# Hybrid decoder layer on one core: a two-tile first weight block on its own queue, and the third out chunk's h transposed on TensorE

## The chip, the cores and the metric

One core of one Trainium2 chip runs the kernel. The metric is the device time in microseconds (us) of one execution; the time given for a kernel is the median of several runs. Five engines work side by side: TensorE (PE in the profile; PEld is its weight load), VectorE (DVE), ScalarE (ACT), GpSimd (POOL) and SyncE (SP), which here only issues DMAs. All transfers run on the 16 DMA engines of the core.

## The reference

One decoder layer on x of 256 tokens by 2048 channels, float32: forgetting attention (16 heads of 128) behind an RMS norm, then a gated MLP with a causal convolution of width 3 behind another.

```python
h = x
a = rms_norm(h, mix_norm)                      # h * rsqrt(mean(h*h) + eps) * gain
q, k, v, f_logit = split(a @ fox_w_in)         # 2048 -> 3 * 2048 + 16
...
h = h + attention(q, k, v, f_logit) @ fox_w_out
up = rms_norm(h, ffn_norm) @ ffn_w_up          # 2048 -> 2 * 5632
y = causal_conv3(up)
gate, val = split(y)
h = h + (silu(gate) * val) @ ffn_w_down        # 5632 -> 2048
```

## The kernel before

Every matmul runs on split operands: a float32 number is taken as hi + lo, both of a type that TensorE multiplies at full rate, and three products hi\*hi, hi\*lo and lo\*hi are added up in PSUM. `split_load` (L157) makes this of a weight block: one DMA on SP's queue into `raw` (4 buffers), a cast on ScalarE to `hi` (L167), a subtraction on VectorE to `lo` (L168; 5 buffers each of hi and lo, 1024 columns wide, so two k tiles of 512 columns). `halves` (L214) does the same for activations, with the norm's gain of the channel as a factor: ScalarE (L215), then VectorE (L216). The factor of the RMS norm for each token is applied to the results.

The input side. x stands transposed in memory (`xT`), 16 k tiles of 128 channels by 256 tokens. The first chunk of products, `q0` (heads 12 to 15 of q, 512 columns), walks over the 16 k tiles; its weights come in blocks of 1, 1, 2, 2, ... k tiles (L40). `q_first` runs ahead of each block: it issues the load of the block's x (`x_load`, L193, SP's queue) and makes `xs[k]` from it (`x_make`, L220). The gains of both norms, as 32 columns, come first of all by a DMA on ScalarE's queue (L140). Each k tile has 6 products: for each of two token tiles, hi\*hi (L353), hi\*lo (L354) and lo\*hi (L355). The `k0` chunk follows on the same xs.

The middle. The output projection has four chunks of 512 columns (`out_part`, `out_evac`). Chunk c is added to the residual `res` (L306), and its 512 channels, 4 k tiles of the next norm's input `hs`, must be transposed. For chunks 0 to 2 VectorE transposes blocks of 32 by 32 (L315), 16 DMAs on GpSimd's queue move the blocks (`spread`, L258; 48 in all) into `hT`, and `scale` makes the halves of hs (L324, L325). For chunk 3 `h_turn` (L223) transposes on TensorE (8 transposes of 128 by 128 for the four k tiles, L228, into PSUM), and `halves` reads PSUM. `bg` is a list of such jobs that `tick` takes one from, every second k tile in the out chunks and twice in each quarter of an up half.

The up projection (`up_half`) then has 11 blocks of a gate half (`pug`) and a value half (`puv`), each in four quarters of 4 k tiles: 16 products of 512 columns (L278), then 16 of 256 (L280). Quarter i needs hs[4i] to hs[4i+3]. In the first block the job `spread_rstd` adds a few small products (tile `prb`, L643).

What sets the order: the program gives priorities, and a planner with its own model of durations puts the instructions of each engine into a fixed order (`schedule_with_timeline_sim`). Each engine then runs its list in order, and waits where an input or a buffer isn't ready.

Of the kernel before, what the change touches and what calls it, by code (L numbers as in the profile page):

```python
# [9 lines left out]
F32 = mybir.dt.float32  # L10
F32R = mybir.dt.float32r
AF = mybir.ActivationFunctionType
ALU = mybir.AluOpType
AX = mybir.AxisListType

P = 128
S = 256
SQ = 32
NT = S // P
D = 2048  # L20
KT = D // P
# [7 lines left out]
HEL = 1024  # L29
# [6 lines left out]
def plan_in():  # L36
    r = {}
    for g, (h0, nh) in enumerate(GROUPS):
        q, k, v = (list(range(m * D + h0 * HD, m * D + (h0 + nh) * HD)) for m in range(3))
        r[f"q{g}"] = (q, [1, 1] + [2] * 7 if g == 0 else [4] * 4)  # L40
        r[f"k{g}"] = (k, [4] * 4)
        if g == 0:

            r["v0a"] = (v[0 : 2 * HD] + list(range(3 * D, 3 * D + NH)), [6, 6, 4])
            r["v0b"] = (v[2 * HD :], [8, 8])
        else:
            r[f"v{g}"] = (v, [4] * 4)
    return r
# [46 lines left out]
def trunk_kernel(  # L95
# [1 line left out]
    tc: tile.TileContext,  # L97
    x: bass.AP,
    xT: bass.AP,
    cols: bass.AP,  # L100
    g_qk: bass.AP,
    w_in: bass.AP,
    b_f: bass.AP,
# [6 lines left out]
    nc = tc.nc  # L110
# [13 lines left out]
    bg = deque()  # L124
# [12 lines left out]
    make_identity(nc, ident)  # L137

    gains = const.tile([P, 2 * KT], F32, name="gains")
    nc.scalar.dma_start(gains, cols)  # L140
    gmix, gffn = gains[:, 0:KT], gains[:, KT : 2 * KT]
    gqk = const.tile([P, 2 * HD], F32, name="gqk")
    neghalf = const.tile([P, 16], F32, name="neghalf")
# [12 lines left out]

    def split_load(src, kk, n, name):  # L157
        raw = wraw.tile([P, WEL], F32, tag="raw", name=f"raw_{name}")
        nc.sync.dma_start(raw[:, 0 : kk * n], src)
        hv, lv = [], []  # L160
        step = max(1, HEL // n)
        for j in range(0, kk, step):
            w = min(step, kk - j)
            hi = whi.tile([P, HEL], F32R, tag="hi", name=f"hi_{name}_{j}")
            lo = wlo.tile([P, HEL], F32R, tag="lo", name=f"lo_{name}_{j}")
            src = raw[:, j * n : (j + w) * n]
            nc.scalar.copy(hi[:, 0 : w * n], src)  # L167
            nc.vector.tensor_tensor(  # L168
                lo[:, 0 : w * n], src, hi[:, 0 : w * n].bitcast(F32), op=ALU.subtract
            )  # L170
            hv += [hi[:, i * n : (i + 1) * n] for i in range(w)]
            lv += [lo[:, i * n : (i + 1) * n] for i in range(w)]
        return hv, lv
# [5 lines left out]
    xs = [acts.tile([P, 2, S], F32R, tag=f"as{k}", name=f"xs{k}") for k in range(KT)]  # L179
# [6 lines left out]
        nc.gpsimd.tensor_tensor(dst, dst, neghalf[:, 0:cols], op=ALU.pow)  # L186

    xv = x.rearrange("o (t p) d -> p (o t) d", p=P)
    xTv = xT.rearrange("p (k s) -> p k s", s=S)
    xq = [acts.tile([P, 2, S], F32, tag=f"os{i}", name=f"xq{i}") for i in range(KT // 2)]  # L190

    def x_load(k, w):
        nc.sync.dma_start(xq[k // 2][:, k % 2 : k % 2 + w, :], xTv[:, k : k + w, :])  # L193


    def res_load(c, late):
# [17 lines left out]
    def halves(dst, src, g):  # L214
        nc.scalar.activation(dst[:, 0, :], src, AF.Copy, scale=g)  # L215
        nc.vector.scalar_tensor_tensor(  # L216
            dst[:, 1, :], src, g, dst[:, 0, :].bitcast(F32), op0=ALU.mult, op1=ALU.subtract,
        )

    def x_make(k):  # L220
        halves(xs[k], xq[k // 2][:, k % 2, :], gmix[:, k : k + 1])

    def h_turn(kp):  # L223
        pt = bank(f"ht{kp}")
        for j in range(2):
            for t in range(NT):
                k = 2 * kp + j
                nc.tensor.transpose(  # L228
                    pt[:, j * S + t * P : j * S + (t + 1) * P], res[:, t, k * P : (k + 1) * P], ident,
                )  # L230
        for j in range(2):
            k = 2 * kp + j
            halves(hs[k], pt[:, j * S : (j + 1) * S], gffn[:, k : k + 1])
# [69 lines left out]
    def out_evac(pts, c):  # L303
        for t in range(NT):
            hc = res[:, t, c * 512 : (c + 1) * 512]
            nc.vector.tensor_tensor(hc, hc, pts[t], op=ALU.add)  # L306
            sq = hp_.tile([P, 512], F32, tag="hsq", name=f"hsq{c}_{t}")
            square(sq, t, c)
        if c == 3:
            bg.extend([nop, lambda: [h_turn(kp) for kp in (6, 7)]])  # L310
            return
        hq = tp.tile([P, 4 * NT, P], F32, tag="hq", name=f"hq{c}")
        hT = tp.tile([P, NT, 4, P], F32, tag="hT", name=f"hT{c}")
        for t in range(NT):
            nc.vector.transpose(  # L315
                hq[:, 4 * t : 4 * t + 4, :].rearrange("p k s -> p (k s)"), res[:, t, c * 512 : (c + 1) * 512]
            )
        spread(hT.rearrange("p t k s -> p (t k) s"), hq, nc.gpsimd)

        def scale():  # L320
            for j in range(4):
                k = 4 * c + j
                g, d = gffn[:, k : k + 1], hs[k].rearrange("p a (t s) -> p a t s", t=NT)
                nc.scalar.activation(d[:, 0], hT[:, :, j, :], AF.Copy, scale=g)  # L324
                nc.vector.scalar_tensor_tensor(  # L325
                    d[:, 1], hT[:, :, j, :], g, d[:, 0].bitcast(F32), op0=ALU.mult, op1=ALU.subtract,
                )

        bg.extend([nop] * (4, 3, 6)[c] + [scale])

    with tc.tile_pool(name="att", bufs=2) as att, tc.tile_pool(name="ckp", bufs=1) as ckp:
        scr = dram.tile([NH, S], F32, name="scr")
# [4 lines left out]
        def chunk(name, pre=None):  # L337
            cols, kbs = plan[name]
            n = len(cols)
            pts = [bank(f"p{name}_{t}", "mm") for t in range(NT)]  # L340
            k0 = 0
            lv = None
            for bi, kk in enumerate(kbs):
                if pre:
                    pre(bi, lv)
                hv, lv = split_load(wi[name, k0], kk, n, f"{name}_{bi}")
                for j in range(kk):
                    k = k0 + j
                    for t in range(NT):
                        o = pts[t][:, 0:n]  # L350
                        ah = xs[k][:, 0, t * P : (t + 1) * P]
                        al = xs[k][:, 1, t * P : (t + 1) * P]
                        nc.tensor.matmul(o, lhsT=ah, rhs=hv[j], start=(k == 0), stop=False)  # L353
                        nc.tensor.matmul(o, lhsT=ah, rhs=lv[j], start=False, stop=False)  # L354
                        nc.tensor.matmul(o, lhsT=al, rhs=hv[j], start=False, stop=(k == KT - 1))  # L355
                    if (k + 1) % (2 if n > 256 else 4) == 0:
                        tick()
                k0 += kk
            last[0] = lv[-1]
            return pts  # L360
# [198 lines left out]
        for g, (h0, nh) in enumerate(GROUPS):  # L559
            qd = {}  # L560
# [6 lines left out]


            def q_first(bi, lv):
                if bi < 2:  # L570
                    x_load(bi, 1)
                    x_make(bi)
                else:
                    k = 2 * (bi - 1)
                    x_load(k, 2)
                    x_make(k)
                    x_make(k + 1)
# [49 lines left out]
    for c in range(2, 4):  # L627
        pts = [bank(f"po_{c}_{t}", "mm") for t in range(NT)]
# [163 lines left out]
```

## Time and profile before

| | us |
|---|---|
| median of 3 runs | 1122.23 (1120.85 to 1123.55) |
| the profiled execution's own time | 1121.05 |
| its span, first to last instruction | 1119.3 |
| TensorE busy in it | 1110.5 (99%) |
| VectorE, ScalarE, GpSimd busy | 753.2, 570.5, 87.6 |

The chain of work that ended last is 96% TensorE. How to read the rows: a timeline row has start, duration, engine, line, operation, output<-inputs, shapes and how many instructions were merged; in brackets the idle time of that engine before it, and what ended it. SPq and ACTq are the queues on which SP and ScalarE issue DMAs. A matmul's duration reaches past the start of the next, since they are pipelined: the price of one in a dense row is the distance of the starts.

### The profile page before, as it was taken

Reading aid. Unit: us, or ns where it says so; the run is one execution under the profiler, and the core shown is the slowest. Engines: PE = TensorE matmul, PEld = TensorE weight load, DVE = VectorE, ACT = ScalarE, POOL = GpSimd, SP = SyncE. Lnnn points to the kernel's source line nnn. Section 1 sums busy time; section 2 is a strip of 40 time slices with the busy share of each in tenths; the row PEclk is TensorE's granted clock in tenths of the full one; section 3 lists DMA queues with packets and bytes.
Section 4 is the critical chain, followed back from the end, with each engine's and each line's share of the span. In section 5 each row is a group of like instructions: output and inputs, shape, how many; then the busy total and the mean of one; then the engine's idle time right before and its main releaser. Section 6 shows DMA issues by size and latency. Waiting matters only on the chain.

```text
span 1119.3 us, 15032 instructions
## 1 busy us (share of the span) xinstructions
PE 1110.5 (99%) x5672; PEld 950.0 (85%) x5672; DVE 753.2 (67%) x1210; ACT 570.5 (51%) x837; POOL 87.6 (8%) x152
## 2 busy tenths in 40 slices
PE   8999999999999999999999999999999999999998
PEld 6898888888888888888888888888888888888886
DVE  6666948677647658687655767765577777557864
ACT  7644545454535656565444555543455554346542
POOL 1102403030106400000000000000000000000000
PEclk9999999999999999999999999999999999999999
DMA  9839577677648645555555555555555555555542
GB/s 336 312 76 357 140 264 224 176 266 209 217 157 239 215 168 188 189 188 190 197 200 171 196 192 192 193 201 188 188 188 188 189 188 193 197 183 183 198 176 75
DMA packets 89145, 223.51 MB, mean 200 GB/s; under 512 B 58624, under 2 KB 58912, under 8 KB 64752
## 3 DMA queue, kind: packets, MB, share of 16 engines
q1 hardware_dynamic: 86640, 218.52, 57.8%
q0 software_dynamic: 2288, 4.01, 1.5%
q8 instruction: 44, 0.72, 0.2%
q14 instruction: 29, 0.24, 0.1%
q10 hardware_dynamic: 144, 0.02, 0.0%
HBM read 212.28 MB, written 2.11 MB: 192 GB/s over the span
## 4 chain that ended last, share of the span: by engine, by line
PE 96%; SPq 1%; DMA 1%; DVE 1%; ACT 0%; issue 0%; DVEq 0%
PE pug L278 14%; PE puv L278 14%; PE puv L280 8%; PE pug L280 7%; PE pd L290 7%; PE pd L289 7%; PE pd L291 7%; PE po L291 3%; PE pk L355 3%; PE pk L354 3%; PE po L290 3%; PE po L289 3%; PE pk L353 3%; PE pq L354 2%; PE pq L355 2%; PE pq L353 2%
## 5 line engine op out<-in xcount | busy, mean ns | idle before, releaser
L278 PE MATMUL puv<-hs,hi_uv 128*128 128x512 f32 x704 | 168.8, 391 | 1.2 <-ACT hi_uv L167 1.1
L278 PE MATMUL pug<-hs,hi_ug 128*128 128x512 f32 x704 | 167.9, 391 | 0.0
L168 DVE TENSOR_TENSOR lo_ug<-raw_ug,hi_ug 128x1024 fp32r<-128x1024 f32 x88 | 106.1, 1221 | 81.1 <-PE puv L280 36.8
L168 DVE TENSOR_TENSOR lo_d<-raw_d,hi_d 128x1024 fp32r<-128x1024 f32 x88 | 106.6, 1223 | 78.6 <-ACT hi_d L167 56.1
L278 PEld LDWEIGHTS puv<-hs,hi_uv 128*128 128x128 f32 x704 | 129.2, 188 | 26.9 <-ACT hi_uv L167 1.6
L278 PEld LDWEIGHTS pug<-hs,hi_ug 128*128 128x128 f32 x704 | 129.6, 188 | 25.2
L167 ACT CAST hi_d<-raw_d 128x1024 fp32r<-128x1024 f32 x88 | 92.2, 1052 | 114.8 <-PE pd L291 83.0
L167 ACT CAST hi_uv<-raw_uv 128x1024 fp32r<-128x1024 f32 x88 | 92.4, 1051 | 106.7 <-PE pug L278 63.2
L167 ACT CAST hi_ug<-raw_ug 128x1024 fp32r<-128x1024 f32 x88 | 92.6, 1052 | 105.9 <-PE puv L278 34.4
L168 DVE TENSOR_TENSOR lo_uv<-raw_uv,hi_uv 128x1024 fp32r<-128x1024 f32 x88 | 106.2, 1221 | 58.5 <-PE pug L280 47.2
L290 PE MATMUL pd<-lo_d,gt 128*128 128x512 f32 x352 | 136.2, 389 | 0.0
L289 PE MATMUL pd<-hi_d,gt 128*128 128x512 f32 x352 | 134.5, 389 | 0.0
L291 PE MATMUL pd<-hi_d,gt 128*128 128x512 f32 x352 | 134.2, 389 | 0.0
L280 PEld LDWEIGHTS puv<-hs,lo_uv 128*128 128x128 f32 x704 | 90.3, 191 | 3.4
L280 PEld LDWEIGHTS pug<-hs,lo_ug 128*128 128x128 f32 x704 | 90.3, 191 | 3.4
L280 PE MATMUL puv<-hs,lo_uv 128*128 128x256 f32 x704 | 91.5, 283 | 0.0
L280 PE MATMUL pug<-hs,lo_ug 128*128 128x256 f32 x704 | 91.3, 283 | 0.0
L291 PEld LDWEIGHTS pd<-hi_d,gt 128*128 128x128 f32 x352 | 66.1, 188 | 13.7
L289 PEld LDWEIGHTS pd<-hi_d,gt 128*128 128x128 f32 x352 | 66.1, 188 | 13.6
L290 PEld LDWEIGHTS pd<-lo_d,gt 128*128 128x128 f32 x352 | 66.1, 188 | 13.6
L168 DVE TENSOR_TENSOR lo_o<-raw_o,hi_o 128x1024 fp32r<-128x1024 f32 x32 | 39.1, 1222 | 34.2 <-ACT hi_o L167 33.8
L168 DVE TENSOR_TENSOR lo_q<-raw_q,hi_q 128x1024 fp32r<-128x1024 f32 (+1 forms) x33 | 38.8, 1187 | 27.0 <-ACT hi_q L167 27.0
(171 smaller groups left out, 1816.7 us busy)
## 6 DMA issues: line engine op xcount, KB each, us to landing
raw_ug<-in_w_up SPq DMA_DIRECT2D x44, 1024.0 KB, 4.9
raw_uv<-in_w_up SPq DMA_DIRECT2D x44, 1024.0 KB, 4.9
raw_d<-in_w_down SPq DMA_DIRECT2D x44, 1024.0 KB, 4.8
raw_k<-in_w_in SPq DMA_DIRECT2D x16, 1024.0 KB, 8.8
raw_o<-in_w_out SPq DMA_DIRECT2D x16, 1024.0 KB, 5.6
raw_q<-in_w_in SPq DMA_DIRECT2D x12, 1024.0 KB, 6.0
raw_v<-in_w_in SPq DMA_DIRECT2D x12, 1024.0 KB, 5.7
raw_q<-in_w_in SPq DMA_DIRECT2D x7, 512.0 KB, 6.8
```

Of the source, the lines that this page charges most:

```text
L167: nc.scalar.copy(hi[:, 0 : w * n], src)
L168: nc.vector.tensor_tensor(lo[:, 0 : w * n], src, hi[:, 0 : w * n].bitcast(F32), op=ALU.subtract)
L278: nc.tensor.matmul(o[:, 0:512], lhsT=hv, rhs=a.rearrange("p a s -> p (a s)"), start=first, stop=False)
L280: nc.tensor.matmul(o[:, 0:S], lhsT=lv, rhs=a[:, 0, :], start=False, stop=last)
L289: nc.tensor.matmul(pts[t], lhsT=ah, rhs=hv, start=first, stop=False)
L290: nc.tensor.matmul(pts[t], lhsT=ah, rhs=lv, start=False, stop=False)
L291: nc.tensor.matmul(pts[t], lhsT=al, rhs=hv, start=False, stop=last)
L353: nc.tensor.matmul(o, lhsT=ah, rhs=hv[j], start=(k == 0), stop=False)
L354: nc.tensor.matmul(o, lhsT=ah, rhs=lv[j], start=False, stop=False)
L355: nc.tensor.matmul(o, lhsT=al, rhs=hv[j], start=False, stop=(k == KT - 1))
```

## The change

The first weight block of `q0` holds two k tiles and comes by ScalarE's queue; it is split one k tile at a time. `xT` now begins with one block of 32 columns of gains and x of k tiles 0 and 1, loaded by one DMA on SP's queue into `xg`; the DMA of the columns is gone, and GpSimd copies them out of `xg`. The halves of `xs[0]` are both made on VectorE. In k tile 0 the products are in the order hi\*hi, lo\*hi, hi\*lo, each for both token tiles. Chunk 2 of the output projection goes the way of chunk 3: no block transposes and no DMAs, but `h_turn(4)` and `h_turn(5)` as a job behind one empty job.

```diff
--- before.py
+++ after.py
@@ -37,7 +37,7 @@
     r = {}
     for g, (h0, nh) in enumerate(GROUPS):
         q, k, v = (list(range(m * D + h0 * HD, m * D + (h0 + nh) * HD)) for m in range(3))
-        r[f"q{g}"] = (q, [1, 1] + [2] * 7 if g == 0 else [4] * 4)
+        r[f"q{g}"] = (q, [2] * 8 if g == 0 else [4] * 4)
         r[f"k{g}"] = (k, [4] * 4)
         if g == 0:
 
@@ -97,7 +97,6 @@
     tc: tile.TileContext,
     x: bass.AP,
     xT: bass.AP,
-    cols: bass.AP,
     g_qk: bass.AP,
     w_in: bass.AP,
     b_f: bass.AP,
@@ -137,7 +136,6 @@
     make_identity(nc, ident)
 
     gains = const.tile([P, 2 * KT], F32, name="gains")
-    nc.scalar.dma_start(gains, cols)
     gmix, gffn = gains[:, 0:KT], gains[:, KT : 2 * KT]
     gqk = const.tile([P, 2 * HD], F32, name="gqk")
     neghalf = const.tile([P, 16], F32, name="neghalf")
@@ -156,9 +154,10 @@
 
     def split_load(src, kk, n, name):
         raw = wraw.tile([P, WEL], F32, tag="raw", name=f"raw_{name}")
-        nc.sync.dma_start(raw[:, 0 : kk * n], src)
+        first = name == "q0_0"
+        (nc.scalar if first else nc.sync).dma_start(raw[:, 0 : kk * n], src)
         hv, lv = [], []
-        step = max(1, HEL // n)
+        step = 1 if first else max(1, HEL // n)
         for j in range(0, kk, step):
             w = min(step, kk - j)
             hi = whi.tile([P, HEL], F32R, tag="hi", name=f"hi_{name}_{j}")
@@ -186,11 +185,14 @@
         nc.gpsimd.tensor_tensor(dst, dst, neghalf[:, 0:cols], op=ALU.pow)
 
     xv = x.rearrange("o (t p) d -> p (o t) d", p=P)
-    xTv = xT.rearrange("p (k s) -> p k s", s=S)
+
+    X0 = 2 * KT + 2 * S
+    x0 = xT[0 : P * X0].rearrange("(p x) -> p x", p=P)
+    xTv = xT[P * X0 :].rearrange("(p k s) -> p k s", p=P, s=S)
     xq = [acts.tile([P, 2, S], F32, tag=f"os{i}", name=f"xq{i}") for i in range(KT // 2)]
 
     def x_load(k, w):
-        nc.sync.dma_start(xq[k // 2][:, k % 2 : k % 2 + w, :], xTv[:, k : k + w, :])
+        nc.sync.dma_start(xq[k // 2][:, k % 2 : k % 2 + w, :], xTv[:, k - 2 : k - 2 + w, :])
 
 
     def res_load(c, late):
@@ -306,8 +308,8 @@
             nc.vector.tensor_tensor(hc, hc, pts[t], op=ALU.add)
             sq = hp_.tile([P, 512], F32, tag="hsq", name=f"hsq{c}_{t}")
             square(sq, t, c)
-        if c == 3:
-            bg.extend([nop, lambda: [h_turn(kp) for kp in (6, 7)]])
+        if c >= 2:
+            bg.extend([nop, lambda: [h_turn(kp) for kp in (2 * c, 2 * c + 1)]])
             return
         hq = tp.tile([P, 4 * NT, P], F32, tag="hq", name=f"hq{c}")
         hT = tp.tile([P, NT, 4, P], F32, tag="hT", name=f"hT{c}")
@@ -326,7 +328,7 @@
                     d[:, 1], hT[:, :, j, :], g, d[:, 0].bitcast(F32), op0=ALU.mult, op1=ALU.subtract,
                 )
 
-        bg.extend([nop] * (4, 3, 6)[c] + [scale])
+        bg.extend([nop] * (4, 3)[c] + [scale])
 
     with tc.tile_pool(name="att", bufs=2) as att, tc.tile_pool(name="ckp", bufs=1) as ckp:
         scr = dram.tile([NH, S], F32, name="scr")
@@ -344,15 +346,18 @@
                 if pre:
                     pre(bi, lv)
                 hv, lv = split_load(wi[name, k0], kk, n, f"{name}_{bi}")
+                if name == "q0" and bi == 0:
+                    pre(-1, lv)
                 for j in range(kk):
                     k = k0 + j
-                    for t in range(NT):
-                        o = pts[t][:, 0:n]
-                        ah = xs[k][:, 0, t * P : (t + 1) * P]
-                        al = xs[k][:, 1, t * P : (t + 1) * P]
-                        nc.tensor.matmul(o, lhsT=ah, rhs=hv[j], start=(k == 0), stop=False)
-                        nc.tensor.matmul(o, lhsT=ah, rhs=lv[j], start=False, stop=False)
-                        nc.tensor.matmul(o, lhsT=al, rhs=hv[j], start=False, stop=(k == KT - 1))
+                    prods = [(t, p) for t in range(NT) for p in ((0, hv), (0, lv), (1, hv))]
+                    if name == "q0" and k == 0:
+                        prods = [(t, p) for p in ((0, hv), (1, hv), (0, lv)) for t in range(NT)]
+                    for t, (a, wv) in prods:
+                        nc.tensor.matmul(
+                            pts[t][:, 0:n], lhsT=xs[k][:, a, t * P : (t + 1) * P], rhs=wv[j],
+                            start=(k == 0 and a == 0 and wv is hv), stop=(k == KT - 1 and a == 1),
+                        )
                     if (k + 1) % (2 if n > 256 else 4) == 0:
                         tick()
                 k0 += kk
@@ -567,11 +572,20 @@
 
 
             def q_first(bi, lv):
-                if bi < 2:
-                    x_load(bi, 1)
-                    x_make(bi)
+                if bi == 0:
+                    qd["xg"] = xg = att.tile([P, 4, S], F32, tag="ckB", name="xg", bufs=1).rearrange("p h s -> p (h s)")
+                    nc.sync.dma_start(xg[:, 0:X0], x0)
+                elif bi == -1:
+                    xg = qd["xg"]
+                    src = xg[:, 2 * KT : 2 * KT + S]
+                    nc.vector.tensor_scalar(xs[0][:, 0, :], src, xg[:, 0:1], None, op0=ALU.mult)
+                    nc.vector.scalar_tensor_tensor(
+                        xs[0][:, 1, :], src, xg[:, 0:1], xs[0][:, 0, :].bitcast(F32), op0=ALU.mult, op1=ALU.subtract,
+                    )
+                    halves(xs[1], xg[:, 2 * KT + S : X0], xg[:, 1:2])
+                    nc.gpsimd.tensor_copy(gains, xg[:, 0 : 2 * KT])
                 else:
-                    k = 2 * (bi - 1)
+                    k = 2 * bi
                     x_load(k, 2)
                     x_make(k)
                     x_make(k + 1)
@@ -762,10 +776,13 @@
 
     laid = {
         "x": a["x"],
-        "xT": a["x"][0].T.reshape(KT, P, S).transpose(1, 0, 2).reshape(P, KT * S),
-        "cols": _np.concatenate(
-            [by_columns(a[n]) for n in ("mix_norm", "ffn_norm")], axis=1
-        ),
+        "xT": _np.concatenate([
+            _np.concatenate(
+                [by_columns(a[n]) for n in ("mix_norm", "ffn_norm")] + [a["x"][0].T[k * P : (k + 1) * P] for k in range(2)],
+                axis=1,
+            ).ravel(),
+            a["x"][0].T[2 * P :].reshape(KT - 2, P, S).transpose(1, 0, 2).ravel(),
+        ]),
         "g_qk": _np.concatenate([a[n].reshape(1, -1) for n in ("fox_q_gain", "fox_k_gain")], axis=1),
         "w_in": by_blocks(a["fox_w_in"][0], blocks_in()),
         "b_f": a["fox_b_f"],
```

## Rows read from the trace of the kernel before

**Rows 1.** Page, part 2: granted TensorE clock in 40 slices of the span
```profile
PEclk9999999999999999999999999999999999999999
```

**Rows 2.** Waits of TensorE over the whole span: total us, times, longest
```profile
PE pq L353 <- ACT hi_q L167: 1.5, 1, 1.5
PE puv L278 <- ACT hi_uv L167: 1.1, 1, 1.1
```

**Rows 3.** Timeline of TensorE, q chunk and first k product: start us, us, engine line
```profile
10.35 0.73 PE L353 MATMUL pq<-hi_q,xs 128*128 128x512 f32 x2 [1.47 <-ACT hi_q L167]
11.61 0.50 PE L354 MATMUL pq<-lo_q,xs 128*128 128x512 f32 x1 [0.52 <-DVE lo_q L168]
...
27.61 0.62 PE L353 MATMUL pq<-hi_q,xs 128*128 128x512 f32 x2
30.34 0.62 PE L353 MATMUL pk<-hi_k,xs 128*128 128x512 f32 x2
```

**Rows 4.** Timeline, ScalarE and VectorE, first 12 us
```profile
3.25 0.51 ACT L215 ACTIVATE xs<-xq,gains 128x256 fp32r<-128x256 f32 x1 [0.52 <-DMA gains<-in_cols]
3.79 0.48 DVE L216 SCALAR_TENSOR_TENSOR xs<-xq,gains,xs 128x256 fp32r<-128x256 f32 x1 [2.58 <-ACT xs L215]
4.73 0.69 DVE L168 TENSOR_TENSOR lo_q<-raw_q,hi_q 128x512 fp32r<-128x512 f32 x1 [0.45 <-ACT hi_q L167]
6.29 0.62 ACT L167 CAST hi_q<-raw_q 128x512 fp32r<-128x512 f32 x1 [0.18 <-DMA raw_q<-in_w_in]
9.25 1.04 ACT L167 CAST hi_q<-raw_q 128x1024 fp32r<-128x1024 f32 x1 [0.34 <-DMA raw_q<-in_w_in]
10.33 1.22 DVE L168 TENSOR_TENSOR lo_q<-raw_q,hi_q 128x1024 fp32r<-128x1024 f32 x1 [0.90 <-ACT hi_q L167]
```

**Rows 5.** Timeline of TensorE, first and second up block
```profile
382.76 3.79 PE L278 MATMUL pug<-hs,hi_ug 128*128 128x512 f32 x16
395.67 0.61 PE L643 MATMUL prb<-ident,rh 128*128 128x128 f32 x4
398.67 2.11 PE L278 MATMUL puv<-hs,hi_uv 128*128 128x512 f32 x8 [1.14 <-ACT hi_uv L167]
...
430.36 3.82 PE L278 MATMUL pug<-hs,hi_ug 128*128 128x512 f32 x16
474.89 3.82 PE L278 MATMUL pug<-hs,hi_ug 128*128 128x512 f32 x16
```

**Rows 6.** Tiles ht and hT: count, ns min/median/max, first and last start
```profile
L228 PE MATMUL ht<-ident,res x8: 272/272/273, 388.3 to 389.1; 128*128 128x128 f32 x8
...
L258 POOL DMA_DIRECT2D hT<-hq x48: 582/582/622, 342.2 to 376.3; - x48
L324 ACT ACTIVATE hs<-hT,gains x12: 493/497/507, 362.2 to 399.7; 128x256 fp32r<-128x256 f32 x12
```

**Rows 7.** Timeline of ScalarE in the first up block
```profile
397.57 1.04 ACT L167 CAST hi_uv<-raw_uv 128x1024 fp32r<-128x1024 f32 x1 [3.46 <-PE puv L278]
398.52 1.71 ACT L324 ACTIVATE hs<-hT,gains 128x256 fp32r<-128x256 f32 x4
```

**Rows 8.** Timeline, first DMA issues (SPq, ACTq) and the warm copy
```profile
0.81 0.40 ACTq L140 DMA_DIRECT2D gains<-in_cols  x1
0.81 0.39 SPq L193 DMA_DIRECT2D xq<-in_xT  x1
2.54 0.19 ACT L206 COPY warm<-ones 128x1 f32<-128x1 f32 x1
3.14 0.44 SPq L159 DMA_DIRECT2D raw_q<-in_w_in  x1
```

**Rows 9.** DMA view, 0 to 40 us: GB/s, one number per microsecond
```profile
GB/s 0 16 236 300 96 346 346 338 356 379 428 406 420 406 395 395 418 410 401 447 434 344 221 418 410 295 410 340 225 184 324 397 379 408 401 393 387 436 406 411
```

**Rows 10.** DMA issues of the same 40 us: KB each, median us to landing
```profile
raw_q<-in_w_in SPq DMA_DIRECT2D x7, 512.0 KB, 6.8
raw_q<-in_w_in SPq DMA_DIRECT2D x2, 256.0 KB, 3.4
```

## The prediction

> **What bounds the kernel now.** I read the page first, then the waits of TensorE, then its timeline at the two places that the change touches. The granted clock is 1.00 in every slice of the span, which is the upper of the two levels, 2.4 GHz [rows 1]; so no stage is slowed by the clock, and a microsecond of missing matmul is a microsecond of the span. In the list of what TensorE waited for there are only two places of note: the first q chunk and the first up block (the puv line) [rows 2]. Everything else runs matmul behind matmul. So the change can give something only at the start and around the first up block, and each instruction that it adds to TensorE costs its full price.
>
> **Loss at the start.** The q chunk has 16 k tiles of 6 products, 96 in all. Two k tiles (12 products) lie between the starts at 27.61 and 30.34 us, so one product takes 2.73/12 = 0.2275 us, and 96 take 21.8 us. The k chunk starts at 30.34 [rows 3], so the q chunk behaves as if a dense train had begun at 30.34 - 21.8 = 8.5 us. What fixes that 8.5 is read from the same rows: two k tiles (12 products) and the two first products of the third were done before 11.61, when the 15th product started, and it waited for a lo. 11.61 - 14 x 0.2275 = 8.4. So it isn't the first product that counts (it starts at 4.75), but the lo halves of k tiles 2 and 3. Their chain: the raw block landed at 9.25 (ScalarE had waited for that DMA), the cast took 1.04, VectorE began at 10.33 and took 1.22 [rows 4].
>
> **Loss in the first up block.** Block 0 runs from its first product at 382.76 to block 1 at 430.36, 47.60 us. Block 1 runs from there to 474.89, 44.53 us. Block 0 has 12 extra TensorE instructions: 8 transposes for k tiles 12 to 15, and 4 of the tile prb [rows 5]. The transposes start 0.11 us apart (8 from 388.3 to 389.1) [rows 6]; 12 x 0.11 = 1.32. The rest, 47.60 - 44.53 - 1.32 = 1.75 us, is lost. Where: TensorE took half a block of the val part (puv) before the third quarter of the gate part, out of program order, and then stood 1.14 us for its next hi [rows 5]. On ScalarE that cast waited 3.46 us for a buffer held by puv, and behind it in the same queue stood the four scale instructions that make k tiles 8 to 11 of hs [rows 7]. They are the third out chunk's; gate k tiles 8 to 11 could start only after them.
>
> **The change, part by part.**
> *Third out chunk.* Removed: two VectorE block transposes, a third of the 48 DMAs that GpSimd issues at 0.58 us, and four ScalarE scale instructions that read the tile hT at 0.50 us with four on VectorE [rows 6]. TensorE waits for none of them in the fourth out chunk, so their time is hidden and I count nothing for it. Added: 8 transposes on TensorE at 0.11, +0.88 us on the path, and eight halves from PSUM of about the same length as the eight removed. They are put behind the second tick of the fourth out chunk, 4 k tiles or 5.4 us after its start; what is queued behind them on TensorE is the rest of that chunk, and it would wait only if the two PSUM banks or the chunk's sum were late, for which no row shows a sign. hs 8 to 11 is then ready some 15 us before the up block begins, so the gate part has no reason to be left, and the 1.75 us go. I count all of it, because block 1, which has everything ready, loses nothing. What is late next is hs 12 to 15, still turned in block 0's first quarter and needed in its fourth, two quarters later (44.53/8 = 5.6 us each). Sum of this part: -1.75 + 0.88 = -0.87 us.
>
> *Start.* Up to and including k tiles 2 and 3, before: the columns, x in 128, 128 and 256 KB, weights in 256, 256 and 512 KB, 1552 KB. After: one 272 KB transfer (columns and x 0, 1), 256 KB of x, and two of 512 KB of weights: 1552 KB again. So no byte is saved. What differs is the issue: the weights of k tiles 2 and 3 were SP's sixth issue, at 3.14 us; now they are its third, at about 1.7 (two slots of 0.46 behind 0.81), and the first weight block goes out on ScalarE's queue at 0.81 in the slot of the columns [rows 8]. The line of DMA rates per microsecond shows why that may help: 300 GB/s in the fourth, 96 in the fifth, about 340 in the sixth [rows 9]. A hole worth 0.7 us lies between the first transfers and those issued later. With twice the bytes queued at 0.81 I take it as gone: block k 2, 3 lands at 9.25 - 0.7 = 8.6 instead of 9.25. Bounds: 9.25 (same bytes, same engines) and 7.9 (another 0.7 from the earlier issue).
> The second condition is the first block. Call T the time when both its transfers (784 KB) have landed. Before, the first 784 KB of the stream landed at 6.29, where the second cast waited for its DMA [rows 4]; without the hole 5.6. 512 KB transfers took a median of 6.8 us to land in this stretch, behind a queue, 256 KB 3.4 [rows 10]; that bounds T by 0.81 + 3.4 = 4.2 and 0.81 + 6.8 = 7.6. I take 5.8. After T, VectorE has to make: the hi of x 0 (no row shows that operation on VectorE; 0 and 0.69 bound it, I take 0.48, as its sibling), lo of x 0 to x 3 at 0.48, two weight lo at 0.69, and the lo of k tiles 2 and 3 at 1.22 [rows 4]: 5 x 0.48 + 2 x 0.69 + 1.22 = 5.0. ScalarE's part (two casts of 0.62, three of 0.50, one of 1.04) is shorter, 3.8, and runs beside it. So the train can begin at T + 5.0 - 14 x 0.2275 = T + 1.8 = 7.6; by the landing of k 2, 3 at 8.6 + 1.04 + 1.22 - 3.2 = 7.7. The later holds, against 8.4 before: -0.7 us. With the bounds it is between -1.4 (k 2, 3 at 7.9) and +1.0 (T at 7.6). The reordered products of k tile 0 and GpSimd's copy of the columns lie in the wait before the train and cost nothing; without that cover they would cost one GpSimd copy, 0.2 us.
>
> **Sum.** -0.87 - 0.7 = -1.6 us. The profiled execution took 1121.05, so it would take 1119.5; it lies 1.2 below the median of the runs, 1122.23, and against that median the forecast is 1120.6. A difference of 0.2%, 2.2 us, is about what a measurement can tell from no change; single runs of before already lie 1.4 below and 1.3 above their median.
>
> **The rivals.**
> *The second queue brings nothing.* Both queues feed the same DMA engines; if these and not the issue are the limit, k tiles 2 and 3 land at 9.25 as before, the train stays at 8.4, and only the out chunk's part is left: -0.9, 1121.4. For it: the stream runs at 340 to 430 GB/s from the sixth microsecond on [rows 9]. Against it: the hole in the fifth. The Trainium skill, "DMA: Bandwidth & Descriptors", section "Issuing engines are not separate DMA queues", says this as a rule: transfers from several engines interleave on the same engines and a second issuer saves only issue time. The trace so far agrees for all but that hole.
> *The start gives more.* The hole goes and the earlier issue counts in full (T about 5.4, k 2, 3 at 7.9): -1.4 - 0.87 = -2.3, 1119.9.
> *The first block is late (slower).* TensorE now starts only when one large pair of transfers is in, and the weight block shares the engines with what SP queues behind its own. If ScalarE's issue comes after its table load and warm copy, which end at 2.73 [rows 8], or if 512 KB takes its 6.8 us, T is 7.6 or more and the train starts at 9.4: +1.0. It decides from T = 7.5 on, where it eats the 0.87 of the other part; at T = 8 it is +1.4 - 0.87, 1122.8. Against it: the columns' DMA on the same queue was issued at 0.81, ahead of the table load.
> *The change does not do what it says to the up block.* Instruction order on each engine comes from a planner; if it still takes puv early, or another wait appears there, the 0.88 is paid and nothing returns: +0.88 - 0.7 = +0.2, 1122.4. Against it: k tiles 8 to 11 were the only late input.
>
> **How the numbers follow.** Forecast as worked out 0.43; start gives more 0.20; second queue brings nothing 0.19; first block late 0.10; up block unchanged 0.08. The likeliest gives 1120.6. The range reaches down to the second case less the 1.4 by which a run lies below its median, 1118.5, and up to the slow cases at 1122.6, with the worst of the first block left out. Faster by over 0.2% needs 2.2 us: most of the second case and a quarter of the first by scatter, 0.32. Slower by over 0.2% only the far end of the late first block, 0.06. The rest, 0.62, is within 0.2%.
>
> **What would show it.** First pk product at 29.6 instead of 30.34; a landing of the first weight block near 5.8 and of the second near 8.6; no hole in the DMA rates of the fifth microsecond; 16 ht transposes instead of 8, 8 of them within the fourth out chunk; no wait of puv for hi_uv, and block 0 at about 45.9 us in place of 47.60. The prediction is wrong if the pk chunk starts after 30.3, or if block 0 still takes over 47.

## The result, and the profile after

The changed kernel took 1129.73 us in the median of six runs (1127.28 to 1130.65), the kernel before 1121.7 in six (1120.27 to 1123.55): ratio 1.0067, 95% interval 1.0051 to 1.0082. It is slower by about 8 us. The forecast was 1120.6 with a range up to 1122.6; it was wrong in sign and missed the range. The profiled execution took 1130.65, the longest of the six; its span is 1128.9.

Page of the changed kernel, part 2, its granted clock by slices, and part 4, the chain that ended last by engine:
```profile
PEclk9999989999999999999999999999999999999999
...
PE 94%; SPq 2%; DVE 2%; DMA 1%; issue 0%; ACT 0%; DVEq 0%
```
Against [rows 1] one slice is new: the sixth, 141 to 169 us, is below the full clock. And the chain now runs 2% of the span, some 20 us, over SP's issuing. The waits of TensorE over the whole span (total us, times, longest):
```profile
PE pq L357 <- ACT hi_q L166: 3.0, 2, 1.9
PE sc L477 <- DMA T<-ksb: 2.7, 1, 2.7
PE pw L214 <- DVE zeros L211: 1.3, 1, 1.3
PE pq L357 <- DVE lo_q L167: 1.2, 1, 1.2
```
The puv wait of [rows 2] is gone, as forecast. New is the second row: scores waiting for a turned k. So I laid the starts of the same products side by side in the two timelines of TensorE, and in those of the experiments below. "Start" is the first pk product; "group 2" runs from the first pv product of head group 1 to the first pk product of group 2 and holds group 2's q chunk; "out" runs from the first out-chunk product to the up block; all in us.

| kernel | start | group 2 | out | block 0 | span |
|---|---|---|---|---|---|
| before | 30.34 | 48.86 | 93.71 | 47.60 | 1119.3 |
| after | 30.16 | 59.51 | 94.60 | 45.84 | 1128.9 |
| e1 | 30.32 | 57.76 | 93.72 | 47.61 | 1127.9 |
| e2 | 29.46 | 48.87 | 94.61 | 45.84 | 1118.4 |
| e3 | 30.54 | 49.51 | 94.61 | 45.84 | 1119.3 |
| e4 | 30.49 | 48.87 | 94.60 | 45.84 | 1118.3 |
| e5 | 30.00 | 57.80 | 93.72 | 47.60 | 1127.8 |
| e6 | 30.15 | 55.75 | 94.61 | 45.83 | 1125.1 |
| e7 | 28.68 | 48.87 | 94.61 | 45.84 | 1116.5 |
| e8 | 30.60 | 52.94 | 94.61 | 45.84 | 1122.6 |
| e9 | 30.24 | 49.62 | 94.61 | 45.84 | 1119.1 |
| e10 | 29.73 | 53.40 | 94.61 | 45.84 | 1122.4 |
| e11 | 30.22 | 48.87 | 94.61 | 45.84 | 1119.7 |
| e12 | 28.93 | 48.86 | 94.61 | 45.83 | 1116.7 |
| e13 | 28.39 | 49.62 | 94.61 | 45.84 | 1117.2 |
| e14 | 30.08 | 48.87 | 94.61 | 45.84 | 1117.8 |

Before to after: start -0.18, from there to group 1's pv -0.52, group 2 +10.65, out +0.89, block 0 -1.76, the rest nothing: +9.08, and the last product ends up 9.09 later (the medians differ by 8.0). **All of the loss lies in 60 us of the attention, which the diff does not touch.** What happened there shows on SP's queue. Timeline of SP, kernel before (start us, length us, issues):
```profile
115.96 11.42 SPq L258 DMA_DIRECT2D T<-qsb  x16
127.49 0.54 SPq L159 DMA_DIRECT2D raw_q<-in_w_in  x1
128.13 11.14 SPq L258 DMA_DIRECT2D pT<-s  x16
139.37 1.50 SPq L159 DMA_DIRECT2D raw_q<-in_w_in  x3
140.96 16.25 SPq L258 DMA_DIRECT2D T<-ksb  x16
```
and of the changed kernel:
```profile
116.00 9.44 SPq L260 DMA_DIRECT2D T<-qsb  x13
125.54 10.52 SPq L260 DMA_DIRECT2D pT<-s  x16
136.11 1.92 SPq L260 DMA_DIRECT2D T<-qsb  x3
138.13 10.39 SPq L260 DMA_DIRECT2D T<-ksb  x16
148.62 2.51 SPq L158 DMA_DIRECT2D raw_q<-in_w_in  x4
```
The planner wrote another order for SP. The four weight blocks of group 2's q chunk, issued at 127.49 and 139.37 before, come behind all 48 small transposing transfers (0.65 to 0.73 us of issue each) and go out at 148.62. TensorE's list differs too: group 1's 16 scores stand 60 products earlier, ahead of that q chunk (they start at 149.96, before at 161.41). The timeline of TensorE:
```profile
149.96 0.77 PE L477 MATMUL sc<-T,T 128*128 128x128 f32 x2 [2.73 <-DMA T<-ksb]
...
151.37 0.63 PE L477 MATMUL sc<-T,T 128*128 128x128 f32 x2
151.80 1.06 PE L478 MATMUL sc<-T,T 128*128 128x256 f32 x2
...
153.48 0.38 PE L477 MATMUL sc<-T,T 128*128 128x128 f32 x2
153.70 0.60 PE L478 MATMUL sc<-T,T 128*128 128x256 f32 x2
156.19 1.04 PE L357 MATMUL pq<-hi_q,xs 128*128 128x512 f32 x2 [1.89 <-ACT hi_q L166]
158.46 0.79 PE L357 MATMUL pq<-lo_q,xs 128*128 128x512 f32 x1 [1.23 <-DVE lo_q L167]
159.05 0.63 PE L357 MATMUL pq<-hi_q,xs 128*128 128x512 f32 x1
159.48 0.63 PE L357 MATMUL pq<-lo_q,xs 128*128 128x512 f32 x1
...
163.53 0.39 PE L357 MATMUL pq<-lo_q,xs 128*128 128x512 f32 x1
163.76 0.40 PE L357 MATMUL pq<-hi_q,xs 128*128 128x512 f32 x1
```
The waits add up to 5.85 us, not 10.65. The other 4.80 is pace, which fell twice. After the first wait a pair of scores of 128 columns takes 0.43 us (151.37 to 151.80), from 153 on 0.22 (153.48 to 153.70). After the next two waits products of 512 columns start 0.43 us apart (159.05 to 159.48) until 163.5, then 0.23. The table of stretches shows the granted clock beside it (after the busy times of PE, weight loads, VectorE, ScalarE and GpSimd: clock, DMA share, GB/s):
```profile
140.00:145.00 5.00, 5.00 (x26) 4.22 (x25) 0.85 (x2) 0.74 (x2) 0.00 (x0) 1.00 0.36 53
145.00:150.00 5.00, 2.27 (x14) 1.84 (x12) 0.85 (x2) 2.08 (x4) 0.00 (x0) 0.96 0.52 66
150.00:155.00 5.00, 4.30 (x16) 3.49 (x16) 2.42 (x15) 1.67 (x7) 2.36 (x8) 0.70 0.84 324
155.00:160.00 5.00, 2.58 (x6) 1.56 (x7) 4.96 (x17) 4.77 (x10) 0.91 (x3) 0.64 0.99 415
160.00:165.00 5.00, 5.00 (x17) 3.94 (x16) 5.00 (x11) 3.09 (x7) 1.25 (x3) 0.68 1.02 424
```
It fell behind the 2.73 us in which TensorE stood, and again around the waits of 1.89 and 1.23 us; a pace of 0.43 against 0.23 is the lower level, 1.2 GHz, against 2.4. The Trainium skill, "TensorE: Matmul & The Clock Gate", section "Wait — 56ns, not 53.3ns?", gives 426.7 ns between starts of 512 columns at that level; the trace agrees with 0.43.

The out chunks and the up block did what was forecast. Timeline of TensorE (answers to [rows 5]) and tile ht (to [rows 6]):
```profile
393.61 3.79 PE L280 MATMUL pug<-hs,hi_ug 128*128 128x512 f32 x16
...
439.45 3.82 PE L280 MATMUL pug<-hs,hi_ug 128*128 128x512 f32 x16
```
```profile
L230 PE MATMUL ht<-ident,res x16: 270/272/273, 376.4 to 399.9; 128*128 128x128 f32 x16
```
Block 0 takes 45.84 us, forecast 45.9; 16 transposes, the first 8 in the fourth out chunk.

In this pair of profiles the start moved by 0.18 us; three profiles of one and the same start differ by 0.9 (last section). Timeline of ScalarE (answers to [rows 4]) and DMA view of 2 to 8 us (bytes per slice of 0.15 us, then queues: packets, MB, share of the engines' time), changed kernel:
```profile
5.07 0.51 ACT L217 ACTIVATE xs<-xg 128x256 fp32r<-128x256 f32 x1 [2.34 <-DMA xg<-in_xT]
5.48 1.12 ACT L166 CAST hi_q<-raw_q 128x512 fp32r<-128x512 f32 x2
...
8.99 1.05 ACT L166 CAST hi_q<-raw_q 128x1024 fp32r<-128x1024 f32 x1 [1.58 <-DMA raw_q<-in_w_in]
```
```profile
GB/s 322 73 182 96 153 212 289 294 331 422 322 484 449 362 470 372 330 410 382 423 519 369 410 413 239 31 0 0 0 0 0 0 0 82 137 109 191 382 437 328
...
q0 software_dynamic: 32, 0.01, 26.9%
```
The first block was in by 5.5 (forecast 5.8), but the weights of k tiles 2, 3, issued at 1.72 as forecast, landed at 8.99, not 8.6. The hole of [rows 9] in the fifth microsecond is not there; there is one in the seventh. The last row is GpSimd's queue, whose one transfer here is the 8 KB broadcast of the forget gate's bias; it has 26.9% of the engines' time, in the same 6 us of the kernel before 1.5%. That made it the suspect.

### The profile page after: what moved, and what is told of

Same layout as the page of the kernel before. It is cut to its first block, busy times and chain, and to the rows that moved or that the text cites. A ratio compares the mean times of both kernels' runs of the same rounds, so it can differ in the third digit from the quotient of the medians.

```text
span 1128.9 us, 15022 instructions
## 1 busy us (share of the span) xinstructions
PE 1116.0 (99%) x5680; PEld 954.8 (85%) x5680; DVE 752.3 (67%) x1209; ACT 570.8 (51%) x836; POOL 73.4 (7%) x137
## 4 chain that ended last, share of the span: by engine, by line
PE 94%; SPq 2%; DVE 2%; DMA 1%; issue 0%; ACT 0%; DVEq 0%
PE puv L280 14%; PE pug L280 14%; PE pq L357 8%; PE puv L282 7%; PE pug L282 7%; PE pd L291 7%; PE pd L292 7%; PE pd L293 7%; PE pk L357 6%; PE pv L357 4%; PE po L291 3%; PE po L293 3%; PE po L292 3%; SPq L260 2%; PE pv0a L357 1%; PE pv0b L357 1%
## 5 line engine op out<-in xcount | busy, mean ns | idle before, releaser
L357 PE MATMUL pq<-hi_q,xs 128*128 128x512 f32 x256 | 83.6, 406 | 3.0 <-ACT hi_q L166 3.0
L357 PE MATMUL pk<-hi_k,xs 128*128 128x512 f32 x256 | 80.1, 390 | 0.0
```

The source lines that it names most:

```text
L357: nc.tensor.matmul(pts[t][:, 0:n], lhsT=xs[k][:, a, t * P : (t + 1) * P], rhs=wv[j], start=(k == 0 and a == 0 and wv is hv), stop=(k == KT ...
```

## The experiments

**Which part of the change costs the time: e1 and e2.** e1 is the changed kernel with the third out chunk as before; e2 the kernel before with the new out chunk alone, the reverse of this edit:
```diff
-        if c >= 2:
+        if c == 3:
...
-        bg.extend([nop] * (4, 3)[c] + [scale])
+        bg.extend([nop] * (4, 3, 6)[c] + [scale])
```


> The start as in the changed kernel, the third out chunk as before. Theory A (the new start makes the planner put the second head group's weight loads behind the small transposing DMAs on SP's queue, and TensorE starves around 147 to 164 us): the loss is here in full, the first up block's 0.9 us gain is not, so 1130.6 us, with a wait of sc for T of about 2.7 us. Rival B (the loss comes with the transposes of the third out chunk): 1121.5 us and no such wait.

> The third out chunk transposed on TensorE, the start as before. Theory A: no change up to the out chunks, block 0 of the up projection 45.8 us in place of 47.6, 8 more transposes at 0.11: 0.9 us faster than before, 1120.8 us. Rival B: 1129 to 1130 us.

e1: 1129.57, ratio 1.0078 (1.0063 to 1.0093), group 2 takes 57.76, with a wait of 2.3 us for turned k, and the puv wait is back. e2: 1120.40, ratio 0.9998 (0.9989 to 1.0006), group 2 takes 48.87. The loss comes wholly with the start. The stages "out" and "block 0" of e2 sum to -0.86; the stretch from group 2's k chunk to the out chunks is 0.78 longer than before, with a wait of 0.53 us for a turned p at 188.78, so that most of it doesn't reach the total.

**The order alone: e3 and e4.** e3 changes how many empty background jobs stand ahead of the scores (one more in group 0), e4 sends the transposing transfers of p through GpSimd's queue:
```diff
-            wait = [nop] * (0 if g == len(GROUPS) - 1 else 2)
+            wait = [nop] * (3, 2, 2, 0)[g]
```
```diff
-                sg[:, 0:nh, :].rearrange("p h (m s) -> p (h m) s", s=P),
+                sg[:, 0:nh, :].rearrange("p h (m s) -> p (h m) s", s=P), nc.gpsimd,
```


> The changed kernel with one more empty job ahead of the first head group's scores, which puts the second group's transposing DMAs and the third's weight loads on SP's queue back in the order of before. Theory A: the stall around 147 to 164 us is gone and the clock stays at 1.00: 1120.5 to 1121.0 us, below before. Rival C (the new start itself costs the 8 us, by its two queues or its cold matmuls): 1129 to 1130 us as the changed kernel.

> The changed kernel with the 16 DMAs per head group that transpose the attention weights issued by GpSimd and not by SP, no extra job. Theory A (SP's list is what starves TensorE): the weight loads are no longer behind them, 1120.5 to 1122 us. Rival D (the order of TensorE's own list, scores ahead of the q chunk, is the cause whatever SP does): still 1125 us or more.

e3: 1121.18, ratio 1.0005 (0.9995 to 1.0014), so not below before, where theory A had put it; weight blocks ahead of the 16 transfers of k again, group 1's scores back behind 60 products of the q chunk, clock 1.00. e4: 1119.90, ratio 0.9993 (0.9984 to 1.0002). Both undo the loss with the new start in place. In e4 TensorE's list changed as well (group 1's scores stand behind 81 products of the q chunk), so it does not by itself tell SP's order from TensorE's.

**The loss without the change: e5.** In the kernel before, group 2's weights are held until group 1's k is turned:
```diff
         raw = wraw.tile([P, WEL], F32, tag="raw", name=f"raw_{name}")
+        if name[:3] == "q2_":
+            nc.gpsimd.tensor_copy(raw[:, 0:1], gate[0][:, 0, 0, 0:1])
...
+            if g == 1:
+                gate[0] = kT
```


> The kernel before with its own start and its own out chunks; only the four weight blocks of head group 2's q chunk are tied (by a one-column copy on GpSimd from group 1's turned k) to the end of group 1's 16 small k transfers, so that on SP's queue they come behind these, as in the changed kernel. Theory A (the loss is those weights standing behind the small transfers, wherever the start comes from): first pv product of group 1 to first pk product of group 2 grows from 48.9 to 57-60 us, TensorE waits for turned k, hi_q and lo_q of 1 to 3 us each near 150-160 us, granted clock 0.6 to 0.8 in the slices after them, total 1129 to 1132; pk at 29.5 to 30.5 and block 0 at 47.6 as before. Rival E (something in the new start itself, such as the columns' copy or the tile that x 0, 1 share with the attention's broadcast, disturbs the attention later): no such loss, 48.9 us, total 1120.5 to 1122.5.

1130.83, ratio 1.0088 (1.0073 to 1.0102); group 2 takes 57.80. Its waits of TensorE:
```profile
PE sc L475 <- DMA T<-ksb: 3.3, 1, 3.3
PE pq L356 <- ACT hi_q L169: 2.1, 2, 1.7
PE pq L357 <- DVE lo_q L170: 2.1, 2, 1.5
```
These are the three waits of the changed kernel, with the old start. (The second and third rows each hold a short wait at the start as well; in group 2 the waits are 3.29, 1.67 and 1.54, 6.50 of the 8.94 us lost, and the clock fell after the first alone.) With the weights late the planner also drew group 1's scores 60 products ahead, as it had in the changed kernel: that is a consequence of the late weights. Theory A holds, and nothing in the new start disturbs the attention but through the order (E falls).

**Only the weights moved: e6.** SP's order of the small transfers stays as in the changed kernel:
```diff
-        (nc.scalar if first else nc.sync).dma_start(raw[:, 0 : kk * n], src)
+        (nc.scalar if first else nc.gpsimd if name[:2] == "q2" else nc.sync).dma_start(raw[:, 0 : kk * n], src)
```


> The changed kernel; only the four weight blocks of head group 2's q chunk are issued on GpSimd's queue in place of SP's. SP's order of the small transfers in this stretch stays as in the changed kernel (13 of turned q, 16 of turned p, 3 of turned q, 16 of turned k). Theory A (the loss is the weights behind the small transfers): it goes, 48.9 us from pv of group 1 to pk of group 2, total 1120.0 to 1121.8, granted clock 1.00. Rival F (the loss is the order of the small transfers themselves: the turned k lands too late for the scores): TensorE still waits 2 us or more for the turned k, 52 us or more, total 1124 or more.

1126.86, ratio 1.005 (1.0033 to 1.0067): A as the whole cause falls, and F has the size but names the wrong transfer. The weights were in time, the scores went back to their place, but TensorE stood ahead of the products that read the turned p of group 0. Timeline of SP and of TensorE, and the stretch behind it:
```profile
125.88 14.01 SPq L260 DMA_DIRECT2D pT<-s  x16
```
```profile
144.57 1.19 PE L518 MATMUL po<-pT,vsb 128*128 128x256 f32 x2 [3.88 <-DMA T<-qsb]
```
```profile
145.00:150.00 5.00, 5.00 (x15) 4.04 (x15) 0.85 (x2) 1.11 (x3) 0.00 (x0) 0.50 0.33 49
```
With the weights under way on GpSimd's queue the 16 issues of p took 14.01 us instead of 10.52, the products of p started 3.88 us late, and the clock fell to its lower level: 6.9 us lost, of which the wait itself is 3.88. (The profile names the three transfers of turned q that SP issued behind p as what ended the wait. These products read p and not q, so I read it as a wait for that queue; which of its transfers held them is not shown.) So the stretch has more than one deadline behind one queue, weights and small transfers; whichever comes last costs.

**The start: e7 to e11.** e7 is e4 with the bias broadcast moved behind the q/k gains' load (e8 does this with the start of the kernel before and the new out chunk, e9 on top of e3, e11 on top of e2):
```diff
-    nc.gpsimd.dma_start(bfb, b_f.to_broadcast([P, NH]))
...
+        nc.gpsimd.tensor_copy(bfb[:, 0:1], late[:, 0:1].bitcast(F32))
+        nc.gpsimd.dma_start(bfb, b_f.to_broadcast([P, NH]))
```


> The changed kernel with group's p spread on GpSimd as in e4, and the broadcast of the forget gate's bias (GpSimd, issued at 1.5 us, not needed before the v chunk) moved behind the q/k gains' load. Theory G (this broadcast's packets hold up the DMA engines at the start, and that is why the new start gave nothing): no microsecond with DMA under 50% between 3 and 9 us, the first x block lands by 4.4 instead of 5.07, weights of k tiles 2, 3 by 8.3 instead of 9.0, pk at 29.4 to 29.8 instead of 30.2 to 30.5, total 1119.0 to 1119.6. Rival H (the engines or the memory are the limit at the start, the broadcast only shows late): landings within 0.2 us of those of the changed kernel, pk at 30.2 to 30.5, total 1119.7 to 1120.5.

> The start of the kernel before, with the third out chunk's h transposed on TensorE (as e2), p spread on GpSimd (as e4) and the broadcast of the forget gate's bias moved as in e7. Theory G: the hole in the fifth microsecond goes here too, weights of k tiles 2, 3 land by 8.6 instead of 9.25, pk at 29.2 to 29.7, total 1118.7 to 1119.5. Rival H: pk at 29.5 to 30.3 (the two values that this start has shown), total 1119.8 to 1120.6. e7 against e8 is the new start against the old one with the rest alike: by the forecast 0.7 us for the new one, by what was seen so far within 0.3.

e7: 1118.17, ratio 0.9975 (0.9965 to 0.9985), start 28.68: **faster than both kernels**. Its DMA view has no hole, its weights of k tiles 2, 3 are there before ScalarE asks for them:
```profile
GB/s 102 85 278 214 302 307 220 378 378 335 389 307 458 486 347 384 399 410 355 355 369 369 355 355 328 382 328 382 396 423 423 355 423 451 382 396 341 328 451 328
```
```profile
7.59 1.05 ACT L165 CAST hi_q<-raw_q 128x1024 fp32r<-128x1024 f32 x1
```
G holds, with more gain than it asked for (start 28.68 for 29.4 to 29.8) and one miss: the x block still landed at 5.1. e8: 1123.92, ratio 1.0022 (1.0009 to 1.0035), a miss for both theories: start 30.60, and a 2.23 us wait for the turned p in group 2 (52.94). So p on GpSimd is not safe by itself: e4 and e7 have no such wait, e8, with another order, has it.

> As e3 (the changed kernel, one more empty background job before head group 0's scores, p spread on SP) with the broadcast of the forget gate's bias moved as in e7. If the gain of e7 at the start is that move alone, pk starts at 28.5 to 28.9 (e7: 28.68, e3: 30.54), pk to po stays at e3's 258.8, total 1119.0 to 1120.0 against e3's 1121.18. If the gain needs p on GpSimd's queue, pk stays at 30.2 to 30.6 and the total at 1120.5 to 1121.5.

> As e9, but the first weight block goes out on SP's queue, behind the first x block, in place of ScalarE's. Forecast's theory (the second queue saves issue time, one slot of 0.46 us for each transfer behind it): first block and weights of k tiles 2, 3 land 0.4 to 0.7 us later than in e9, pk at 29.0 to 29.5, total 0.4 to 0.7 above e9's. Rival (transfers of both queues share the same engines, the second queue brings nothing): pk within 0.15 of e9's, total within 0.3.

> As e2 (the start of the kernel before, third out chunk's h on TensorE, p spread on SP) with the bias broadcast moved. Theory: the old start is limited by the issue of its many transfers on SP, so the move gives little: weights of k tiles 2, 3 land at 8.9 to 9.3, pk at 29.4 to 30.6, total 1119.5 to 1120.8. If instead the broadcast was what held up the old start too: pk at 28.5 to 29.2, total 1118.5 to 1119.3. In both cases 48.9 us from pv of group 1 to pk of group 2: if it is 52 or more as in e8, the loss there came from the bias's move and not from p on GpSimd's queue.

e10 sends the first weight block back to SP's queue. e9: 1119.93, 0.9985 (0.9976 to 0.9994); e10: 1120.14, 0.9988 (0.9979 to 0.9997); e11: 1121.43, 1.0 (0.9991 to 1.0008). e11 agrees with its theory in the start (30.22; weights of k tiles 2, 3 at 9.10): the old start gains nothing from the move, and with p on SP the loss of e8 is gone; its total is 0.6 above the range given. The second queue is worth 0.2 us between the medians of e9 and e10, whose intervals overlap. With one queue (e10) the weights of k tiles 2, 3 landed at 8.05, in e9 by 7.41: that much the issue counts, as the forecast had it. The price of two queues shows in the x block, which landed at 3.60 in e10 and 5.15 in e9, and the first k product of e10 is 0.5 earlier, where one theory had it later and the other unmoved. That two queues share the engines and that a second one saves issue time alone is the rule of the Trainium skill that the prediction named ("DMA: Bandwidth & Descriptors", section "Issuing engines are not separate DMA queues"); here the two landings agree with it.

(e10's profiled execution is the slowest of its eleven, 1124.09, with a 2.7 us wait in group 2 ahead of the products of p; e9's has 0.5 there. In this order p seems to be at its deadline.) e9's profile was unlike e7's: no hole, yet a start of 30.24. Its profiled execution took 1120.79, 0.9 above its median, so this start need not be that of its other runs. The first products of e9, then of e7, in the timeline of TensorE:
```profile
6.22 2.07 PE L358 MATMUL pq<-hi_q,xs 128*128 128x512 f32 x4 [1.18 <-ACT hi_q L165]
8.09 1.05 PE L358 MATMUL pq<-lo_q,xs 128*128 128x512 f32 x2
```
```profile
6.18 1.21 PE L358 MATMUL pq<-hi_q,xs 128*128 128x512 f32 x4 [1.35 <-ACT hi_q L165]
7.22 0.63 PE L358 MATMUL pq<-lo_q,xs 128*128 128x512 f32 x2
```
Four products take 1.87 us in e9 and 1.04 in e7: the lower and the upper level. (The granted clock reads 1.00 in both, so here only the pace shows it.)

**Pace or landing: e12, e13, e14.** e7, e9 and e4, with more warm-up matmuls, so that TensorE does not stand ahead of its first product:
```diff
-    for i in range(4):
+    for i in range(7):
         nc.tensor.matmul(pw[:, 0:256], lhsT=zeros[:, 0:P], rhs=zeros, start=True, stop=True)
```


> As e7, with 7 in place of 4 warm-up matmuls ahead of the first product, so that TensorE is not idle between the warm-up (ends near 5) and the first product (near 6.2). Theory W (in the new start the first 8 to 11 products run at half pace, 0.43 us apart, because TensorE had not come up to its upper clock level or lost it while it stood; e7's profiled execution escaped that by chance): products 0.23 us apart from the first or second on, pk at 28.5 to 28.9 in the profile, total 1117.6 to 1118.2, and the runs of this kernel lie closer together than e7's 1117.8 to 1119.3. Rival L (the pace of the first products does not count, the lo of k tiles 2, 3 does): pk and total as e7's, within 0.3. If the three extra matmuls delay the first product: pk up to 0.5 later.

> As e9 (extra job, bias later, p on SP) with 7 warm-up matmuls. e9's profile has 11 products at half pace up to 11 us and pk at 30.24. Theory W: full pace from the start, pk at 28.5 to 29.0, total 1118.3 to 1119.0 against e9's 1119.93. Rival L: pk at 30.0 to 30.4, total 1119.6 to 1120.2.

> As e4 (the changed kernel with p spread on GpSimd, the bias broadcast where it was) with 7 warm-up matmuls; so e4, e7, e12 and this are the four cases of bias early or late and 4 or 7 warm-ups. Two obstacles, either of which alone is enough (the landing of k tiles 2, 3, held up by the broadcast, and the pace): first products 0.23 us apart, but the lo of k tiles 2, 3 still late, waits of 1 us or more for it, pk at 29.8 to 30.4, total 1119.4 to 1120.0, as e4's 1119.90. If the pace alone was the term: pk at 28.6 to 29.2, total 1118.0 to 1118.7.

e12: 1118.02, ratio 0.997 (0.9959 to 0.9981), its runs within 0.6 us of each other (e7's within 1.4). e13: 1119.43, 0.9979 (0.9971 to 0.9988), start 28.39 against e9's 30.24; its total came 0.4 above what W gave, 0.5 below e9's. e14: 1119.86, 0.999 (0.9981 to 0.9999), start 30.08. First products of e14:
```profile
6.17 1.21 PE L357 MATMUL pq<-hi_q,xs 128*128 128x512 f32 x4
...
10.05 0.73 PE L357 MATMUL pq<-hi_q,xs 128*128 128x512 f32 x2 [0.82 <-ACT hi_q L166]
11.31 0.50 PE L357 MATMUL pq<-lo_q,xs 128*128 128x512 f32 x1 [0.53 <-DVE lo_q L167]
```
Full pace, and still late: with the early broadcast the landing of k tiles 2, 3 sets the start by itself (e4, e14: 30.49, 30.08). Moving the broadcast is worth 1.25 to 1.84 us between medians (e3 to e9, e4 to e7, e14 to e12). That pace matters when the broadcast is gone rests on one pair of profiles (e9 30.24, e13 28.39). Between medians three more warm-up matmuls bring 0.5 us there and 0.15 from e7, whose profile had full pace without them, to e12; the intervals overlap. So the landing is shown as an obstacle, the pace as one that some executions meet.

## Why the prediction was wrong

**The out chunk: right.** Forecast -1.75 + 0.88 = -0.87; measured -1.76 + 0.89. Where it was looked for (16 transposes, no puv wait, block 0 at 45.9) it stands.

**What failed is the sum, by what it left out.** The step is "-0.87 - 0.7 = -1.6 us": the start is counted by what it does to the train, and nothing behind it has a term; the order of all later work was taken as given. It knew that a planner orders each engine's instructions, but named it only in the rival on the up block, with 0.08, and priced that at +0.2. The term it lacked is the 60 us of group 2, +10.65: 5.85 of waits and 4.80 of lower clock. e5 gives the loss without the change, e3 and e4 the change without the loss. In the changed kernel's list group 0's scores had slipped 26 products and more (93.19 us instead of 87.47), and the planner's order of the next 60 us came out another way. The same slip stands in e3 and e4, which lose nothing, so it is not enough by itself. Why the planner chose that order for this start is not settled; that one empty job turns it back suggests that the two orders lay near each other. Neither of the two signs of being wrong that the prediction gave came true (k chunk after 30.3, block 0 over 47): both looked at the places that the change touches.

**The pace.** The prediction read "a microsecond of missing matmul is a microsecond of the span" from a clock of 1.00 everywhere [rows 1]. That holds in the kernel before, where TensorE hardly stands. Where it stood 2.73 us the clock went with it, and waits of 5.85 us cost 10.65.

**The start: right that a hole costs, wrong in its cause.** The term of -0.7 us measured -0.18. The prediction took the hole in the fifth microsecond for a gap in the issue, and so for gone with twice the bytes queued. In the changed kernel there is one two microseconds later, and it went only with the bias broadcast moved (e7): landing 8.99, near the upper bound 9.25, not 8.6. With the broadcast moved the cast ran at 7.59, earlier than the lower bound of 7.9. T was right (at most 5.5 against 5.8). And the train was worked out at 0.2275 us per product from its first product on; after 1.09 us of standing the first eight of the changed kernel started 0.44 apart (6.14 to 9.69). Of the rivals "the second queue brings nothing" came true for the start; "the first block is late" did not. One rival has a slip in its sum: with T at 5.4 the start gives T + 1.8 = 7.2 and so -1.2, not -1.4.

## What to carry to other kernels

Where a planner or scheduler writes the order of each engine, a local edit can move the order of an in-order queue far away: compare the whole lists before pricing the edit, and look for stretches where one queue carries both many small transfers and the next stage's weights. A wait of a few microseconds on TensorE may cost nearly twice its length in time. Look for signs of being wrong outside the places that the edit touches. When a repaired bottleneck gives nothing, look for a second one at the same time of arrival (here the weights held up behind the broadcast) before giving the repair up: e12, the changed kernel with three small edits, is 0.3% faster than the kernel before.

## What the runs showed of the hardware that I had not expected

- An 8 KB broadcast on GpSimd's software queue, under way beside large transfers, had 26.9% of the DMA engines' time in 6 us, with seven slices of 0.15 us without a byte moved behind it; in the kernel before it took 1.5%. That moving it closes the hole is shown (e7); how so small a transfer empties the engines is not.
- TensorE's clock fell after single waits of 2.23 (e8: 4.07 us lost), 2.3 (e1), 2.7 (e10), 2.73 (after), 3.29 (e5) and 3.88 us (e6: 6.9 lost); after waits of 0.4 and 0.5 us (e3, e9) it did not. Between these it went both ways: it fell a second time around waits of 1.89 and 1.23 us (after) and held after 1.67 and 1.54 (e5).
- The first pk product of the kernel before, of e2 and of e5, whose starts are the same program, stood at 30.34, 29.46 and 30.00: 0.9 us apart, about as much as the gain that was looked for. The starts of single profiles in the table differ by less than this in several places, and there only totals decide.
